# Hybrid attention block: a finer estimate behind the order of the work, deeper pipelines and a new order of the weight tiles

## Chip, core and metric

The kernel runs on one core of a Trainium2 chip. The metric is the device time of one launch in microseconds: the median of three runs. Each profile is one execution of its own; its span runs from the first to the last instruction of the program, and the launch has some 2 us around it.

## What is computed

One block of a hybrid network, in float32, on 512 tokens of width 1024. The input is normalised and multiplied by one wide weight matrix; the product feeds four mixers of width 512, whose gated outputs are multiplied by an output matrix, added to the input and normalised.

```
h = _rmsnorm(x, norm_g)
p_fox, p_ssm, p_nsa, p_mem = _split(h @ w_in, ...)
mem_kv = _rmsnorm(mem, mem_norm_g) @ w_mem_kv
o = concat([_fox_mixer(p_fox), _ssd_mixer(p_ssm), _nsa_mixer(p_nsa), _mem_mixer(p_mem, mem_kv)])
return _rmsnorm(x + o @ w_out, final_norm_g)
```

"Fox" is causal attention of 8 heads with a decay per token. "SSM" is a chunked state-space scan behind a short convolution. "NSA" is causal attention of 8 heads in three branches (compressed, selected and window blocks; with 512 tokens each of the last two covers all earlier keys) under a relative bias. "Mem" is attention of 4 heads over 256 memory tokens. In fox and NSA a softmax row block of 128 queries has 128, 256, 384 or 512 keys.

## The kernel before, in words

**Tiles.** The weights come as 75 tiles of 128x1024 floats, one DMA of 512 KB each on SP's queue. ACT rounds a tile to a high part (`wh`), POOL subtracts it to get the low part (`wl`), and TensorE multiplies high by high, high by low and low by high (`three`, L544). A projection tile is 24 matmuls of 512 columns into one PSUM bank (`pj`, in `tile_a`, L701). `raw`, `wh` and `wl` are rings of three buffers each (L31).

**Mixers.** Each mixer is a `Pipe` (L331): a list of steps and, for each step, stages. Fox has 16 steps (4 head pairs by 4 query blocks), NSA 32 (the two heads of a pair apart). Their stages are: `s1`, the scores and the softmax (TensorE to `pS` and `pW`, DVE, ACT); `s2`, DVE transposes 32x32 blocks inside a tile (`flip`, L1017); `s2o`, four DMAs for each tile write it to DRAM with the blocks turned (`flip_out`, L1030, tiles `fl` to `far`); `s2i`, one DMA for each tile brings it back (`flip_in`, L1043, `far` to `pt`); `s3`, TensorE multiplies `pt` with the values into `pO`; `s4`, DVE gates the result. So a probability tile is turned by way of memory, and TensorE waits for the landing of `pt`. NSA's relative bias also comes by way of memory, once for each of four head pairs: `rows<-rv` from DRAM to DRAM (`spread`, L1146) and `bt<-rows` (`bias_tile`, L1151).

**Order.** There is no run-time scheduler. While the program is written out, `Clock` (L60) keeps an estimated time for each engine; `note` (L126) prices every instruction as it is issued, and `Sched.run` (L301) chooses what to issue next: the first stage, in the order of `PIPES` (L32) and with at most four pipes at once, whose inputs are estimated to be there at TensorE's estimated time; otherwise one step of the next weight tile in `ORDER` (L46), which is the filler. Every engine, SP too, then runs its instructions strictly in that order. If an input comes later than estimated, TensorE stands still, and the filler that could have run stands behind the waiting matmul.

**What `note` counts for a DMA.** It takes 430 ns of SP (720 for a large one to DRAM), then waits its turn on one shared transfer line at 385 GB/s (170 for the large one), and lands 2100 ns later. Any number of DMAs may be under way. A pause of TensorE of over 1700 ns costs 2000 ns more.

**Bounds on running ahead.** A pipe may have `DF`, `DN`, `DM` and `DS` steps (fox, NSA, mem, SSM) between its first and last stage (L26, checked in `Pipe.due`, L342). All share 58 buffers of 128x512 floats (`G`); `RF`, `RM`, `RN`, `RS` (L36) are buffers that projections must leave free for an open pipe. `GF` and `FN` (L29) say at which query blocks the `s3` matmuls are issued: with `FN` of (0, 1, 2, 3), NSA issues block by block. `load` (L425) issues the DMA of a weight tile as soon as the estimated release of its buffer is at most 300 ns ahead of TensorE. `SOON`, `LATER` and `WIDE` (L38) are by how much POOL must be later than DVE before a subtraction goes to DVE.

Of the kernel before, what the change touches and what calls it, by code (L numbers as in the profile page):

```python
# [22 lines left out]
PUMP = 4  # L23
WARM = 12
NL = 3
DF, DM, DN, DS = 7, 3, 6, 3  # L26


GF, FN = 4, (0, 1, 2, 3)  # L29
BACKLOG = 3000  # L30
RAW, RING = 3, 3  # L31
PIPES = "ssm", "cmp", "fox", "pre", "nsa", "mem"  # L32
LAST = 3
ACTIVE = 4

RF, RM, RN, RS = 1, 1, 2, 5  # L36

SOON, LATER, WIDE = 750, 2000, 5750  # L38

TAKES = {"fq": (2, 1), "fk": (2, 1), "fg": (1, 0), "nq": (2, 0), "ng": (1, 0), "z": (1, 0), "mq": (2, 0), "mg": (1, 0),  # L40
         "mk": (1, 0), "ks": (0, 4), "kw": (0, 4), "kc": (1, 1), "vc": (1, 1), "xb": (2, 0), "mv": (4, 0),
# [2 lines left out]
FOX, SSM, NSA, MEM = 0, 2056, 3600, 5416  # L44

ORDER = (  # L46
# [9 lines left out]
)  # L56
KEYS_A = [k for k in ORDER if k[0] not in ("bv", "bc", "mv") and k[0][:2] != "wo"]
# [2 lines left out]
class Clock:  # L60
# [4 lines left out]
    def __init__(self):  # L65
        self.t = dict.fromkeys(("PE", "ACT", "DVE", "POOL", "SP"), 700.0)
        self.dma = 0.0
        self.used = {}
        self.born = {}
        self.port = []  # L70
        self.tiled = False
        self.last = self.landed = 0.0
        self.banks = []

    @staticmethod
# [50 lines left out]
    def note(self, eng, op, a, k):  # L126
        outs = [x for x in (k.get("out", a[0] if a else None), k.get("accum_out")) if self.is_ap(x)]
        ins = [x for x in (*a[(0 if "out" in k else 1):], *[v for n, v in k.items() if n not in ("out", "accum_out")])
               if self.is_ap(x)]
        out = outs[0]  # L130
        start = self.t[eng]
        for x in ins:
            start = max(start, self.at(x, eng))
        for x in outs:
            if not str(x.space).endswith("DRAM"):
                start = max(start, self.at(x, eng, False))
        wide = [x for x in ins if self.size(x) > 1]
        n = max([self.size(x) for x in (out, *wide)])
        port, lag = False, 0
        if eng == "PE":  # L140
            rhs, m = ins[1], self.size(ins[0])
            n = self.size(rhs)
            exact = rhs.dtype == FT and op != "transpose"
            tiled = m <= 64 and exact
            took = max(n * 4 / 2.4, 107) / 2 if tiled else 2 * max(n * 2 / 2.4, 110) if exact else max(n / 2.4 + 13, 110)
            if tiled != self.tiled:
                start += 50 if tiled else 30
                self.tiled = tiled
            if start > self.t[eng] + 1700:
                took += 2000  # L150
        elif op == "dma_start":
            far = self.box(out) == (0, 1, 0, 1) and self.size(out) > 512 * 128
            took = 720 if far else 430
        elif eng == "ACT":
            near = str(wide[0].space).endswith("SB") if wide else True
            took = (110 if near else 55) + 0.83 * n + (305 if "accum_out" in k else 0)
            lag = 95
        elif op == "memset":
            took = 60 + 0.83 * n
        elif eng == "POOL":  # L160
            took = 1000 if n < 16 else 170 + 2.11 * n
            lag = 70
            port = n >= 16
        else:
            near = [x for x in wide if str(x.space).endswith("SB")]
            fast = op in ("tensor_scalar", "tensor_copy") and len(near) == len(wide)
            took = 130 + 0.52 * n if fast else 70 + 1.04 * n
            lag = 85
            if op == "reciprocal":
                took = 70 + 6.4 * n  # L170
            if op == "tensor_tensor_reduce":
                took += 15
                lag = 140
            port = fast or len(near) > 1
        if port:
            start = self.slot(start, took)
        self.t[eng] = start + took
        done = start + took + lag
        if eng == "PE":
            done += self.DRAIN  # L180
        if op == "dma_start":
            nbytes = 4 * self.size(out) * out.ap[0][1]
            self.dma = max(self.dma, done) + nbytes / (170 if took > 430 else 385)
            self.landed = done = self.dma + 2100
            eng = "DMA"
        if op != "dma_start":
            self.last = max(self.last, done)
        for xs, wrote in ((ins, False), (outs, True)):
            for x in xs:
                u = self.used.setdefault(x.name, {})  # L190
                b = self.box(x)
                if wrote:
                    for q in [q for q in u if b[0] <= q[0][0] and q[0][1] <= b[1] and b[2] <= q[0][2] and q[0][3] <= b[3]]:
                        del u[q]
                u[b, eng, wrote] = max(done, u.get((b, eng, wrote), 0.0))
# [135 lines left out]
class Pipe:  # L331
# [10 lines left out]
    def due(self, bg, k):  # L342
        i = self.at[k]
        if i >= len(self.steps) or (k and i >= self.at[k - 1]) or (k == 0 and i - self.at[-1] >= self.depth):
            return math.inf
        t = self.dues.get((k, i), 0.0)
        take = self.takes[k]
        g, b = take(self.steps[i]) if callable(take) else take
        if not bg.room(g + (bg.kept(self) if k == 0 else 0), b):
            return math.inf  # L350
        if k in self.pre:
            keys, tiles = self.pre[k](self.steps[i])
            if any(key not in bg.done for key in keys):
                return math.inf
            t = max(t, bg.clock.ready(tiles()))
        if k == 0:
            t = max(t, max(bg.clock.t["DVE"], bg.clock.t["ACT"]) - BACKLOG)
        return max(t, bg.clock.free_banks(self.banks[k]))

    def run(self, bg, k):  # L360
        i = self.at[k]
# [10 lines left out]
def block_kernel(ctx, tc, I, out):  # L372
# [29 lines left out]
    def PS(name):  # L402
        t = ps.tile([128, 512], FT, name=name, tag="ps", bufs=8)
        clock.bank(t.name)
        return t
# [19 lines left out]
    def load(n, wait=True):  # L425
        while state["load"] < min(n, len(ORDER)):
            i = state["load"]
            free = rings["raw"][1]
            if not wait and free and free[0] > clock.t["PE"] + 300:
                return  # L430
            raw[i] = ring("raw", FT)
            if i < 2:
                for h in range(2):
                    (A if i == h == 0 else Q).dma_start(out=raw[i][:, h * 512:(h + 1) * 512],
                                                        in_=I["wst"][i, :, h * 512:(h + 1) * 512])
            else:
                Q.dma_start(out=raw[i], in_=I["wst"][i])
            state["load"] += 1
# [568 lines left out]
    def rows_by(x, r):  # L1007
        if clock.t["ACT"] + 100 < clock.t["DVE"]:
            A.activation(x, x, AF.Copy, scale=r)
        else:  # L1010
            V.tensor_scalar(out=x, in0=x, scalar1=r, scalar2=None, op0=OP.mult)

    def flips(w):

        return 1 if 2 * w <= 512 else 2

    def flip(tiles, w):  # L1017

        b, per = w // 128, 2 // flips(w)
        made = []  # L1020
        for c in range(0, 2, per):
            t = G("fl", FT, per * w)
            to = t.rearrange("p (j s b x) -> p s b j x", j=4, s=per, b=b)
# [4 lines left out]
        return made, per, w  # L1028

    def flip_out(f):  # L1030
        made, per, w = f
        far = []
        for t in made:
# [7 lines left out]
        return far, per, w  # L1041

    def flip_in(f):  # L1043
        far, per, w = f
        blocks = []
        for m in far:
# [2 lines left out]
            v = t.rearrange("p (i s b x) -> p s b i x", i=4, s=per, b=w // 128)  # L1049
            blocks += [v[:, s, b] for s in range(per) for b in range(w // 128)]  # L1050
        gs.drop(len(far))
        clock.last = clock.landed
        return blocks

    def fox():
# [60 lines left out]
        def p4(s):  # L1116
            return [("fg", s[0])] if s[1] == 3 else [], lambda: []

        return Pipe([(j, b) for j in range(4) for b in range(4)], [s1, s2, s2o, s2i, s3, s4], DF, [2, 0, 0, 0, 1, 0],
                    [(2, 0), (2, 0), (0, 0), (2, 0), (0, 0), (0, 0)], RF, {0: p1, 5: p4})  # L1120

    rv = dr.tile([8, RVW], FT, name="rv")
    rows = [dr.tile([2, 128, RVW], FT, name=f"rows{j}") for j in range(4)]
# [129 lines left out]
    def nsa():  # L1253
# [131 lines left out]
        def p4(s):  # L1385
            return [("ng", s[0])] if s[2] and (s[1] == 3 or s[0] == 3 and LAST == 2) else [], lambda: []

        return Pipe([(j, b, a) for j in range(4) for b in range(4) for a in range(2)], [s1, s2, s2o, s2i, s3, s4],
                    DN, [2, 1, 0, 0, 1, 0], [t1, (2, 0), (0, 0), (2, 0), (0, 0), (2 if LAST == 2 else 0, 0)], RN,
                    {0: p1, 5: p4})  # L1390

    xs = {}
# [53 lines left out]
    pre = []  # L1446
# [433 lines left out]
```

## Time and profile before

| what | value |
|---|---|
| median of three runs | 545.45 us (543.48, 545.45, 547.86) |
| time of the profiled execution | 549.33 us |
| its span | 547.5 us |
| granted TensorE clock, mean over the span | 0.975 |
| TensorE, DVE, ACT, POOL busy | 95%, 67%, 55%, 45% |
| moved by DMA | 90.43 MB |

Every instruction goes through one recording helper, so all of them carry its line, L243, and groups are told apart by the names of their tiles: `pj<-hh,wh` is a projection's matmul, `pt<-far` the DMA that brings a turned tile back. "SPq" is the sequencer of SP, which issues the DMAs. In the lists of waits, "A <- B: total, times, longest" says that A's engine stood still until B was done. Matmuls overlap, so the record of one (390 ns for 512 columns) is longer than the distance to the next (227 ns), and a busy TensorE says little; what counts is its idle time and its clock.

### The profile page before, as it was taken

Reading aid. Unit: us, or ns where it says so; the run is one execution under the profiler, and the core shown is the slowest. Engines: PE = TensorE matmul, PEld = TensorE weight load, DVE = VectorE, ACT = ScalarE, POOL = GpSimd, SP = SyncE. Lnnn points to the kernel's source line nnn. Section 1 sums busy time; section 2 is a strip of 40 time slices with the busy share of each in tenths; the row PEclk is TensorE's granted clock in tenths of the full one; section 3 lists DMA queues with packets and bytes.
Section 4 is the critical chain, followed back from the end, with each engine's and each line's share of the span. In section 5 each row is a group of like instructions: output and inputs, shape, how many; then the busy total and the mean of one; then the engine's idle time right before and its main releaser. Section 6 shows DMA issues by size and latency. Waiting matters only on the chain.

```text
span 547.5 us, 9040 instructions
## 1 busy us (share of the span) xinstructions
PE 519.4 (95%) x2987; PEld 430.2 (79%) x2987; DVE 369.5 (67%) x947; ACT 301.6 (55%) x679; POOL 244.5 (45%) x165
## 2 busy tenths in 40 slices
PE   9999998997999999999998898889999989999995
PEld 5898886886788888877887677778887778878884
DVE  4468698575577777695677778747768668555544
ACT  5754663666466444822346666636556566556333
POOL 3595362333133337757478435213313333263733
PEclk9999998999899999998999999979999999999998
DMA  8772332186476758061227457876865775631303
GB/s 309 299 271 85 116 115 77 27 260 200 119 203 180 227 166 300 39 231 40 77 78 238 142 162 203 249 205 178 248 194 145 225 223 163 198 109 42 113 38 115
DMA packets 70543, 90.43 MB, mean 165 GB/s; under 512 B 26193, under 2 KB 49617, under 8 KB 70497
## 3 DMA queue, kind: packets, MB, share of 16 engines
q1 hardware_dynamic: 70208, 89.40, 52.1%
q8 instruction: 23, 0.38, 0.3%
q10 hardware_dynamic: 288, 0.46, 0.3%
q14 instruction: 24, 0.19, 0.1%
HBM read 71.46 MB, written 20.53 MB: 168 GB/s over the span
## 4 chain that ended last, share of the span: by engine, by line
PE 61%; DVE 16%; DMA 8%; ACT 6%; SPq 4%; issue 3%; POOL 0%; POOLq 0%; DVEq 0%; ACTq 0%
PE pj L243 25%; PE po L243 15%; PE pb L243 6%; PE pO L243 6%; DMA pt<-far 6%; SPq L243 4%; PE pS L243 4%; DVE Rl L243 2%; DVE xs L243 2%; DVE rs L243 2%; ACT pN L243 1%; DMA rows<-rv 1%; DVE ol L243 1%; ACT pF L243 1%; ACT wh L243 1%
## 5 line engine op out<-in xcount | busy, mean ns | idle before, releaser
L243 POOL TENSOR_TENSOR wl<-raw,wh 128x1024 fp32r<-128x1024 f32 (+1 forms) x72 | 172.3, 2397 | 245.2 <-ACT wh L243 201.1
L243 PE MATMUL pj<-hh,wh 128*128 128x512 f32 x352 | 141.4, 402 | 0.0
L243 PE MATMUL pj<-hh,wl 128*128 128x512 f32 x352 | 138.2, 392 | 0.0
L243 PE MATMUL pj<-hl,wh 128*128 128x512 f32 x352 | 138.1, 392 | 0.0
L243 ACT ACTIVATE wh<-raw 128x1024 fp32r<-128x1024 f32 (+1 forms) x72 | 74.1, 1034 | 13.5 <-DMA raw<-in_wst 7.1
L243 PEld LDWEIGHTS pj<-hh,wl 128*128 128x128 f32 x352 | 66.5, 189 | 14.6
L243 PEld LDWEIGHTS pj<-hh,wh 128*128 128x128 f32 x352 | 66.9, 190 | 13.8 <-issue 1.2
L243 PEld LDWEIGHTS pj<-hl,wh 128*128 128x128 f32 x352 | 66.8, 190 | 11.8
L243 ACT ACTIVATE pN<-pN,nm 128x128 f32<-128x128 f32 (+7 forms) x96 | 45.4, 474 | 28.1 <-DVE nm L243 26.6
L243 PE MATMUL po<-wh,oh 128*128 128x512 f32 x96 | 40.1, 418 | 0.0
L243 PE MATMUL po<-wh,ol 128*128 128x512 f32 x96 | 38.1, 397 | 0.0
L243 PE MATMUL po<-wl,oh 128*128 128x512 f32 x96 | 38.0, 396 | 0.0
L243 ACT ACTIVATE pN<-pN,rs 128x128 f32<-128x128 f32 (+3 forms) x32 | 18.0, 564 | 32.4 <-DVE rs L243 32.4
L243 ACT ACTIVATE pF<-pF,nm 128x128 f32<-128x128 f32 (+3 forms) x32 | 17.8, 556 | 30.9 <-DVE nm L243 30.7
L243 DVE TENSOR_SCALAR rs<-sm 128x3 f32<-128x3 f32 x32 | 15.0, 467 | 29.3 <-ACT pN L243 29.3
L243 PE MATMUL pO<-pt,nv 128*64 128x128 f32 x320 | 25.1, 289 | 8.3 <-DMA pt<-far 8.2
L243 DVE TENSOR_TENSOR acc<-acc,po 128x512 f32<-128x512 f32 (+1 forms) x33 | 21.2, 662 | 12.8 <-PE po L243 12.7
L243 PEld LDWEIGHTS pO<-pt,nv 128*64 128x64 f32 x320 | 20.7, 145 | 10.5 <-DMA pt<-far 10.4
L243 DVE STREAM_TRANSPOSE fl<-pN 128x128 f32<-128x128 f32 (+3 forms) x64 | 28.5, 485 | 0.1
L243 DVE CUSTOM_DVE_ANT_0 pN<-pS,bt 128x128 f32<-128x128 f32 (+5 forms) x80 | 22.2, 318 | 8.9 <-PE pS L243 8.1
L243 DVE SCALAR_TENSOR_TENSOR xs<-x,cwh,xs 128x512 f32<-128x512 f32 x24 | 21.1, 879 | 7.8 <-ACT xs L243 7.1
L243 DVE CUSTOM_DVE_ANT_0 pF<-pS,cst 128x128 f32<-128x128 f32 (+3 forms) x32 | 14.4, 482 | 10.9 <-PE pS L243 10.7
(281 smaller groups left out, 1060.6 us busy)
## 6 DMA issues: line engine op xcount, KB each, us to landing
raw<-in_wst SPq DMA_DIRECT2D x73, 512.0 KB, 4.0
far<-fl SPq DMA_DIRECT2D x144, 64.0 KB, 2.5
pt<-far SPq DMA_DIRECT2D x36, 256.0 KB, 4.3
far<-fl SPq DMA_DIRECT2D x96, 48.0 KB, 1.8
pt<-far SPq DMA_DIRECT2D x24, 192.0 KB, 3.4
rows<-rv SPq DMA_DIRECT2D x4, 656.0 KB, 7.2
bt<-rows SPq DMA_DIRECT2D x4, 528.0 KB, 4.6
xn<-in_xn SPq DMA_DIRECT2D x4, 512.0 KB, 7.7
```

Of the source, the lines that this page charges most:

```text
L243: return f(*a, **k)
```

## The change

The instructions that compute are the same, except that some subtractions may move between DVE and POOL and NSA's first query block is multiplied together with the second. The turning still goes by way of memory: the new helper `transposes` (turning on TensorE) is used for widths up to `NARROW`, which is 0, so no step uses it. What changes is:

- the estimate of a DMA: 430 ns of SP for each; it starts only when one of eight lanes is free, taken in turn; data move from 1330 ns after the start, one DMA after the other, at 340 GB/s (less for runs under 512 bytes, 285 for large ones, 235 from DRAM to DRAM); the landing is at the end of that, 1500 ns later for `far` tiles, and the stage after `flip_in` is due another `AFTER` = 500 ns later;
- the estimate of matmuls (a switch between half-width and full-width tiles costs 90 to 100 ns; a pause of TensorE over 1700 ns costs 3300 ns more) and of DVE work that changes partitions;
- `load` waits until the buffer's release is `SLACK` = 1000 ns past;
- depths, reserves and biases, `FN`, the order of the pipes and `ORDER`. The first seven weight tiles stay; the tiles are the same set.

```diff
-DF, DM, DN, DS = 7, 3, 6, 3
+DF, DM, DN, DS = 12, 5, 12, 2
-GF, FN = 4, (0, 1, 2, 3)
+GF, FN = 4, (1, 2, 3,)
-PIPES = "ssm", "cmp", "fox", "pre", "nsa", "mem"
+PIPES = "fox", "pre", "nsa", "ssm", "mem", "cmp"
-RF, RM, RN, RS = 1, 1, 2, 5
-SOON, LATER, WIDE = 750, 2000, 5750
+RF, RM, RN, RS = 3, 2, 3, 5
+SOON, LATER, WIDE = 250, 2750, 8750
+NARROW, AFTER, SLACK = 0, 500, 1000
...
-    ("bv", 0), ("bv", 1), ("bv", 2), ("bv", 3), ("bc", 0), ("bc", 1), ("bc", 2), ("xb", 0), ("fq", 0),
-    ("xb", 4), ("fq", 2), ("fk", 2), ("fk", 1), ("fk", 0), ("xb", 3), ("fq", 1), ("kc", 0), ("xb", 1),
...
+    ("bv", 0), ("bv", 1), ("bv", 2), ("bv", 3), ("bc", 0), ("bc", 1), ("bc", 2), ("fq", 0), ("fq", 3),
+    ("xb", 0), ("fk", 0), ("xb", 5), ("xb", 6), ("z", 3), ("fk", 1), ("z", 2), ("fq", 1), ("fg", 0),
...
-            took = max(n * 4 / 2.4, 107) / 2 if tiled else 2 * max(n * 2 / 2.4, 110) if exact else max(n / 2.4 + 13, 110)
+            took = max(n * 4 / 2.4 + 4, 107) / 2 if tiled else 2 * max(n * 2 / 2.4, 110) if exact else max(n / 2.4 + (16.5 if n >= 500 else 14.5), 110)
             if tiled != self.tiled:
-                start += 50 if tiled else 30
+                start += 90 if tiled else 100
                 self.tiled = tiled
             if start > self.t[eng] + 1700:
-                took += 2000
+                took += 3300
         elif op == "dma_start":
-            far = self.box(out) == (0, 1, 0, 1) and self.size(out) > 512 * 128
-            took = 720 if far else 430
+            took = 430
+            start = max(start, self.lanes.pop(0))
...
-            port = fast or len(near) > 1
+            port = fast or len(near) > 1 and n >= 16
+            if any(self.box(x)[0] != self.box(out)[0] for x in wide):
+                took, lag = took + 90, 12
...
-            nbytes = 4 * self.size(out) * out.ap[0][1]
-            self.dma = max(self.dma, done) + nbytes / (170 if took > 430 else 385)
-            self.landed = done = self.dma + 2100
+            n = out.ap[0][1]
+            for _, c in out.ap[1:]:
+                n *= c
+            run = 4 * min(out.ap[-1][1], ins[0].ap[-1][1])
+            both = str(out.space).endswith("DRAM") and str(ins[0].space).endswith("DRAM")
+            rate = 235 if both else 285 if n > 75000 and run >= 2048 else 340 * min(run, 512) / 512
+            self.dma = max(self.dma, start + 1330) + 4 * n / rate
+            self.landed = done = self.dma + (1500 if any(x.name[:3] == "far" for x in (out, ins[0])) else 0)
+            self.lanes.append(done)
...
-            if not wait and free and free[0] > clock.t["PE"] + 300:
+            if not wait and free and free[0] + SLACK > clock.t["PE"]:
                 return
...
     def flips(w):
...
+        if w <= NARROW:
+            return transposes([t[:, k * 128:(k + 1) * 128] for t in tiles for k in range(b)])
...
     def flip_in(f):
...
-        clock.last = clock.landed
+        clock.last = clock.landed + AFTER
```

More of the change, by code (lines that the diff above doesn't have):

```diff
@@ L71, in __init__ @@
         self.tiled = False
-        self.last = self.landed = 0.0
+        self.last = self.landed = self.sure = 0.0
+        self.lanes = [0.0] * 8
         self.banks = []
@@ L357, in due @@
             t = max(t, max(bg.clock.t["DVE"], bg.clock.t["ACT"]) - BACKLOG)
-        return max(t, bg.clock.free_banks(self.banks[k]))
+        n = self.banks[k]
+        return max(t, bg.clock.free_banks(n(self.steps[i]) if callable(n) else n))
     def run(self, bg, k):
@@ L1011, in rows_by, with transposes @@
             V.tensor_scalar(out=x, in0=x, scalar1=r, scalar2=None, op0=OP.mult)
+    def transposes(blocks):
+        made = []
+        for i in range(0, len(blocks), 4):
+            n = min(4, len(blocks) - i)
+            p = PS("pT")
+            for k in range(n):
+                T.transpose(p[:, k * 128:(k + 1) * 128], blocks[i + k], ident)
+            pt = G("pt", FT, n * 128)
+            evac(pt, p[:, :n * 128])
+            made += [pt[:, k * 128:(k + 1) * 128] for k in range(n)]
+        gs.drop(2)
+        return made
     def flips(w):
@@ L1030, in flip_out @@
     def flip_out(f):
+        if not isinstance(f, tuple):
+            return f
         made, per, w = f
@@ L1043, in flip_in @@
     def flip_in(f):
+        if not isinstance(f, tuple):
+            return f
         far, per, w = f
@@ L1117, in p4 @@
             return [("fg", s[0])] if s[1] == 3 else [], lambda: []
-        return Pipe([(j, b) for j in range(4) for b in range(4)], [s1, s2, s2o, s2i, s3, s4], DF, [2, 0, 0, 0, 1, 0],
-                    [(2, 0), (2, 0), (0, 0), (2, 0), (0, 0), (0, 0)], RF, {0: p1, 5: p4})
+        return Pipe([(j, b) for j in range(4) for b in range(4)], [s1, s2, s2o, s2i, s3, s4], DF, [2, lambda s: s[1] < NARROW // 128, 0, 0, 1, 0],
+                    [(2, 0), (2, 0), (0, 0), lambda s: (2 if s[1] >= NARROW // 128 else 0, 0), (0, 0), (0, 0)], RF, {0: p1, 5: p4})
     rv = dr.tile([8, RVW], FT, name="rv")
@@ L1388, in nsa @@
         return Pipe([(j, b, a) for j in range(4) for b in range(4) for a in range(2)], [s1, s2, s2o, s2i, s3, s4],
-                    DN, [2, 1, 0, 0, 1, 0], [t1, (2, 0), (0, 0), (2, 0), (0, 0), (2 if LAST == 2 else 0, 0)], RN,
+                    DN, [2, 1, 0, 0, 1, 0], [t1, (2, 0), (0, 0), lambda s: (2 if s[1] >= NARROW // 128 else 0, 0), (0, 0), (2 if LAST == 2 else 0, 0)], RN,
                     {0: p1, 5: p4})
```

12 rows, old and new, of the table ORDER are left out of this document.

## The prediction, made before the change was run

> **What bounds the kernel now.** I read the page first, for the engines and the clock, then TensorE's list of waits, then the stretches at half clock, then the DMA issues and the chain around the longest stall. From the page:
>
> ```profile
> span 547.5 us, 9040 instructions
> PE 519.4 (95%) x2987; PEld 430.2 (79%) x2987; DVE 369.5 (67%) x947; ACT 301.6 (55%) x679; POOL 244.5 (45%) x165
> PEclk9999998999899999998999999979999999999998
> ```
>
> TensorE is the bound: busy 519.4 of 547.5 us, all others two thirds or less. The matmuls are given by the work and the change removes none, so only two things can be won: the time in which TensorE stands still, and the slices in which its clock was lowered (the 8s and the 7). What it waits for, from its list of waits:
>
> ```profile
> PE pO L243 <- DMA pt<-far: 11.6, 10, 2.5
> PE pn L243 <- DVE sq L243: 2.1, 1, 2.1
> PE pS L243 <- DVE Rk L243: 1.8, 2, 1.5
> PE pmv L243 <- POOL wl L243: 1.8, 1, 1.8
> PE pT L243 <- DVE pcp L243: 1.7, 2, 1.3
> PE pw L243 <- DVE warm L243: 1.3, 1, 1.3
> PE pS L243 <- DVE Rl L243: 0.6, 2, 0.4
> ```
>
> Without the start (`warm`) these are 11.6 us for turned tiles that land late, and 2.1 + 1.8 + 1.8 + 1.7 + 0.6 = 8.0 us for DVE and POOL. Behind the longer ones the clock falls. The same table of stretches, four of them at half clock, one right after the first for comparison, and the last long stage:
>
> ```profile
> 90.60:97.40 6.80, 6.27 (x17) 0.50 0.07 27
> 97.40:104.20 6.80, 6.80 (x31) 1.00 0.01 2
> 135.00:141.80 6.80, 5.93 (x31) 0.50 0.52 178
> 356.80:363.70 6.90, 5.90 (x41) 0.51 0.58 157
> 247.60:251.00 3.40, 3.40 (x10) 0.50 0.00 0
> 492.00:530.00 38.00, 38.00 (x199) 1.00 0.17 56
> ```
>
> The columns are the length, TensorE's busy time with its matmuls, the granted clock, the DMA share and GB/s. In the first stretch 17 matmuls went through where the next one of the same length has 31. At half clock, half of the busy time is lost: 6.27/2 = 3.1 us, 5.93/2 = 3.0, 5.90/2 = 3.0, 3.40/2 = 1.7, together 10.8 us. The second and third stand behind `pt` (3.0 + 3.0 = 6.0), the first behind `Rk`, the last behind `sq` (3.1 + 1.7 = 4.8). So 11.6 + 8.0 + 10.8 = 30.4 us can be won at most. From 492 us on there is nothing to win: TensorE is busy for 38.00 of 38.00 us at full clock. The stalls themselves, from TensorE's timeline:
>
> ```profile
> 134.65 0.43 PE L243 MATMUL pO<-pt,fv 128*64 128x128 f32 x2 [2.46 <-DMA pt<-far]
> ...
> 247.34 0.24 PE L243 MATMUL pn<-ones,sq 128*128 128x1 f32 x1 [2.07 <-DVE sq L243]
> ...
> 295.46 0.50 PE L243 MATMUL pmv<-wl,mh 128*128 128x512 f32 x1 [1.82 <-POOL wl L243]
> ...
> 354.93 0.43 PE L243 MATMUL pO<-pt,nv 128*64 128x128 f32 x2 [1.06 <-DMA pt<-far]
> 357.80 3.46 PE L243 MATMUL pO<-pt,nv 128*64 128x128 f32 x29 [2.43 <-DMA pt<-far]
> ```
>
> A pause of 2.07 us is followed by 3.4 us at half clock; after one of 1.82 us I find no stretch with a lowered clock. [...]
>
> **Why `pt` is late.** The DMA issues (KB each, median us from issue to landing), then the chain of waits ahead of the stall at 357.80 and SP's own timeline there:
>
> ```profile
> raw<-in_wst SPq DMA_DIRECT2D x73, 512.0 KB, 4.0
> far<-fl SPq DMA_DIRECT2D x144, 64.0 KB, 2.5
> pt<-far SPq DMA_DIRECT2D x36, 256.0 KB, 4.3
> rows<-rv SPq DMA_DIRECT2D x4, 656.0 KB, 7.2
> bt<-rows SPq DMA_DIRECT2D x4, 528.0 KB, 4.6
> ```
>
> ```profile
> 341.65 6.94 DMA rows<-rv
> ...
> 349.98 2.36 SPq L243
> ...
> 352.87 4.89 DMA pt<-far
> ```
>
> ```profile
> 341.65 0.56 SPq L243 DMA_DIRECT2D rows<-rv  x1
> 342.31 6.60 SPq L243 DMA_DIRECT2D far<-fl  x8
> ```
>
> The old estimate has a `pt` of 256 KB land 0.43 + 262144 B/385 GB/s (0.68) + 2.10 = 3.2 us after its issue; the row says 4.3, so TensorE's matmuls on it are placed 1.1 us too early in the median. On top of that SP's queue stands still: eight `far` DMAs behind `rows<-rv` took 6.60 us, the last of them freed when `rows` had landed, and `pt` behind them went out that much later. The old estimate knows no such limit.
>
> **The change part by part**, against the profiled execution (549.33 us, span 547.5).
>
> 1. Later landings, eight lanes. The new estimate of the same `pt` is 1.33 + 262144/340 (0.77) + 1.50 = 3.6, and with the 0.5 of `AFTER` its matmuls are due after 4.1 us, against 4.3. The lanes stop SP in the estimate too. So of the 11.6 us the median lateness of 1.1 falls to 0.2. I take three quarters: 8.7 us (bounds: 0, if other errors set the landings; 11.6). What fills the place is projection matmuls, of which some are left until 492 us (without that cover the whole wait stays). The price is that each tile is held longer, hence the deeper pipes.
>
> 2. The clock behind them. Three quarters of the 6.0 us: 4.5 us (bounds 0 and 6.0).
>
> 3. Stalls on DVE and POOL, 8.0 us and 4.8 us of clock, 12.8 together. The new order is searched with a pause priced at 3.3 us in place of 2.0, close to the 3.0 to 3.1 of the rows, and with dearer DVE work across partitions, which is what `Rk` and `Rl` are. But these waits were in the old search's reach as well. I take half: 6.4 us (bounds 0 and 12.8).
>
> 4. `FN`. NSA's first query block loses its own burst of half-width matmuls, once for each of four pairs. From the timeline:
>
> ```profile
> 318.06 0.40 PE L243 MATMUL po<-wh,ol 128*128 128x512 f32 x1
> 318.39 0.44 PE L243 MATMUL pO<-ct,vcm 96*64 96x128 f32 x4
> 318.66 0.61 PE L243 MATMUL pO<-pt,nv 128*64 128x128 f32 x8
> 319.19 0.50 PE L243 MATMUL po<-wh,oh 128*128 128x512 f32 x1
> 319.53 0.39 PE L243 MATMUL po<-wl,oh 128*128 128x512 f32 x1
> 319.76 0.40 PE L243 MATMUL po<-wh,ol 128*128 128x512 f32 x1
> ...
> 326.08 0.44 PE L243 MATMUL pO<-ct,vcm 96*64 96x128 f32 x4
> 326.35 1.04 PE L243 MATMUL pO<-pt,nv 128*64 128x128 f32 x16
> 327.33 0.34 PE L243 MATMUL pS<-kh,L 128*128 128x160 f32 x1
> ```
>
> Entering costs 318.39 - 318.06 = 0.33 where 0.23 is usual (319.53 to 319.76): 0.10. The burst of 12 takes 0.80, that of 20 takes 1.25, so 0.056 a matmul and 0.13 fixed. The first `po` behind it takes 0.34 against 0.23: 0.11. Together 0.34 us for a burst, four times: 1.4 us (bounds 1 and 2; the matmuls stay).
>
> 5. What the new estimate has too early. A weight tile now lands 1.33 + 524288/285 (1.84) = 3.2 us after its issue, where the row says 4.0 (the old one: 0.43 + 1.36 + 2.10 = 3.9). `rows<-rv` lands after 1.33 + 671744/235 (2.86) = 4.2 against 7.2 (old: 0.72 + 3.95 + 2.10 = 6.8), `bt<-rows` after 1.33 + 540672/285 (1.90) = 3.2 against 4.6. So ACT may stand up to 0.8 us before each `wh`, in front of softmax exponentials in its queue, whose DVE and TensorE successors then wait; POOL's `wl` gets the tile late. `SLACK` adds up to 1.3 us to each load's issue. What covers it: a tile is split two tiles ahead, 24 matmuls of 0.23 us or 5.4 us each. Where the cover is thin, a stall appears like that at 357.80: 2.43 + 3.0 of clock. I take one such, 5.4 us (bounds: 0, cover everywhere; three, 16.2).
>
> 6. Biases. All the `wl` work is on POOL already and a larger `WIDE` keeps it there; `SOON` and `LATER` move some subtractions between two engines with a third or more of their time free. Nothing; uncovered, a few times 0.7 us. `NARROW` of 0 leaves the turning as it is: nothing. Depths and reserves alone run nothing; they let 1 work.
>
> The start up to 42 us has the same seven tiles, and the end from 492 us is full: neither moves.
>
> Sum: -8.7 - 4.5 - 6.4 - 1.4 + 5.4 = -15.6 us, a span of 531.9 and, from 549.33, 533.7 for an execution like the profiled one. The profiled one lies 3.9 us above the median of the runs, 545.45; from that median, 529.9. I predict **530 us**. Its own range, with one stall more or less and half of 3 either way: 521 to 539.
>
> **The rivals.**
>
> *Nearly all stalls go* (0.14). For it: every one of them is an input that the order could have waited for, and filler exists until 492 us. Against it: landings scatter, and no estimate of medians covers them. Time: 545.45 - 30.4 - 1.4 = 514; with a few us left, 517.
>
> *The stalls only move* (0.20). The old order, too, was the best for its estimate, and an order searched hard leans on the estimate wherever that errs. `pt` gets its cover and `wh`, `bt` or DVE lose theirs: terms 1 to 3 give 19.6, and three to four stalls of 5.4 us come in: 545.45 - 19.6 - 1.4 + 16.2 to 21.6 = 541 to 546; I say 543. The same where the finer counts hardly change the order that matters.
>
> *Slower: the pool of 58 buffers fills* (0.14). Twelve NSA steps and twelve fox steps under way, each with up to two tiles, hold up to 48 of 58, beside the operands of the projections; then no projection may start and filler ends in the middle. The estimate sees a full pool but not how late the real engines drain it, since real landings free the buffers. Each time TensorE pauses for a turn of a tile, 2.5 for `far` and 4.3 for `pt`, and loses 3.0 of clock: 9.8 us. It decides from the third time on, with term 1 to 3 won: 545.45 - 19.6 - 1.4 + 3 x 9.8 = 554; I give it 552 to 558. Against it: TensorE's filler lasts to 492 us now, and the reserves went up (1, 1, 2 to 3, 2, 3).
>
> **How the numbers follow.** Forecast 0.52, nearly all 0.14, moved 0.20, pool 0.14. About 1%, 5.5 us, is what can be told from no change: below 540 is faster, above 551 slower. Faster 0.52 + 0.14 = 0.66, same 0.20, slower 0.14. From 516 to 550 lie the forecast, most of the second case and all of the third, over 8 in 10; the bounds of the terms reach from 514 to beyond 555.
>
> **What would show it.** In the changed profile: the wait of `pO` for `pt<-far` down to some 3 us (term 1); at most two or three stretches at half clock ahead of the end, mean clock near 0.985 (terms 2, 3); NSA's first burst of `pO` for each pair has 12 + 20 = 32 matmuls (term 4); `ACT wh` waiting more for `raw<-in_wst` (term 5). It is wrong if `pt` still leads TensorE's waits at 8 us or more, if `wl` or `wh` take its place, or if TensorE pauses for several us with projections held back.

## The result, and the profile after

The changed kernel takes 527.22 us (median of four runs, 526.23 to 528.49), against 546.63 us for the kernel before on the same chip (543.48 to 547.86). The ratio is 0.9655, with a 95% interval of 0.9604 to 0.9705. The profiled execution took 526.90 us with a span of 525.1, 22.4 us less than the span before. The page, in the same rows as before:

```profile
span 525.1 us, 9054 instructions
PE 506.8 (97%) x2987; PEld 422.7 (80%) x2987; DVE 362.3 (69%) x956; ACT 301.7 (57%) x678; POOL 236.7 (45%) x157
PEclk9999999999999999999999999999999999999998
```

The matmuls are as many (2987), and TensorE is still the bound. Its clock is under nine tenths in no slice but the last, in which the matmuls end. TensorE's list of waits after:

```profile
PE pT L255 <- DVE pcp L255: 3.0, 4, 1.4
PE pb L255 <- DVE fv L255: 2.3, 1, 2.3
PE pO L255 <- DMA pt<-far: 2.0, 2, 1.7
PE pj L255 <- POOL wl L255: 1.5, 2, 0.8
PE pw L255 <- DVE warm L255: 1.3, 1, 1.3
PE pmv L255 <- POOL wl L255: 0.9, 1, 0.9
PE pY L255 <- DVE prev L255: 0.4, 1, 0.4
```

The wait for turned tiles went from 11.6 to 2.0 us. The waits for DVE and POOL are as long as they were, 8.1 us in all (8.3 before, with 0.3 us of `pb`), but others: those on `sq`, `Rk` and `Rl` are gone, and a new one of 2.3 us stands in the start. One stretch at half clock is left before the end:

```profile
156.60:160.00 3.40, 3.40 (x14) 0.51 0.43 103
```

It costs 3.40/2 = 1.7 us, where there were 10.8. So of the 22.4 us, 11.6 - 2.0 = 9.6 come from the wait for `pt`, 10.8 - 1.7 = 9.1 from the clock, 0.2 from the other waits. About 1.4 are the four bursts saved by `FN` (below). Some 2 us I cannot place.

### The profile page after: what moved, and what is told of

It is laid out like the page before. It is cut to its first block, busy times and chain, and to the rows that moved or that the text cites. A ratio compares the mean times of both kernels' runs of the same rounds, so it can differ in the third digit from the quotient of the medians.

```text
span 525.1 us, 9054 instructions
## 1 busy us (share of the span) xinstructions
PE 506.8 (97%) x2987; PEld 422.7 (80%) x2987; DVE 362.3 (69%) x956; ACT 301.7 (57%) x678; POOL 236.7 (45%) x157
## 4 chain that ended last, share of the span: by engine, by line
PE 58%; DVE 15%; DMA 12%; issue 5%; ACT 4%; SPq 3%; POOL 2%; POOLq 0%; DVEq 0%; ACTq 0%
PE pj L255 28%; PE po L255 11%; DMA pt<-far 8%; PE pb L255 6%; PE pO L255 4%; ACT pN L255 3%; PE pS L255 3%; SPq L255 3%; DVE rs L255 3%; DVE pN L255 3%; DVE fl L255 2%; DMA raw<-in_wst 2%; POOL wl L255 1%; DMA far<-fl 1%; DVE acc L255 1%
## 5 line engine op out<-in xcount | busy, mean ns | idle before, releaser
L255 DVE TENSOR_SCALAR rs<-sm 128x3 f32<-128x3 f32 x32 | 16.3, 509 | 28.3 <-ACT pN L255 28.3
L255 DVE TENSOR_TENSOR acc<-acc,po 128x512 f32<-128x512 f32 (+1 forms) x33 | 21.0, 662 | 11.9 <-PE po L255 11.7
L255 DVE RECIPROCAL rs<-sm 128x2 f32<-128x2 f32 x24 | 4.0, 166 | 25.4 <-ACT pF L255 16.7
L255 PEld LDWEIGHTS po<-wh,ol 128*128 128x128 f32 x96 | 18.0, 188 | 4.1
L255 PEld LDWEIGHTS po<-wh,oh 128*128 128x128 f32 x96 | 18.1, 188 | 3.3 <-issue 0.3
```

The lines of the kernel that those rows point to most:

```text
L255: return f(*a, **k)
```

## The experiments

All times are medians; the ratio is to runs of the kernel before on the same chip, with its 95% interval. "pt" is TensorE's wait for `pt<-far`, "others" the rest of its list of waits without `warm`, both in us.

| run | what it is | time | ratio | pt | others |
|---|---|---|---|---|---|
| before | | 546.6 | 1 | 11.6 | 8.3 |
| changed | | 527.2 | 0.9655 [0.9604, 0.9705] | 2.0 | 8.1 |
| e1 | before + new estimate | 532.2 | 0.9682 [0.9634, 0.9730] | 2.1 | 11.2 |
| e2 | changed, old estimate | 540.9 | 0.9844 [0.9801, 0.9888] | 13.2 | 4.4 |
| e3 | changed, old DMA prices | 539.7 | 0.9830 [0.9769, 0.9891] | 11.7 | 4.0 |
| e4 | changed, old depths | 543.4 | 0.9878 [0.9822, 0.9935] | 2.8 | 16.7 |
| e5 | before + turned tiles due 1.5 us later | 545.1 | 0.9936 [0.9914, 0.9959] | 7.7 | 12.4 |
| e6 | changed, no lanes | 540.9 | 0.9854 [0.9817, 0.9892] | 6.7 | 10.2 |
| e7 | changed, old load rule | 523.5 | 0.9547 [0.9519, 0.9575] | 0 | 8.7 |
| e8 | changed, old order of tiles | 537.4 | 0.9800 [0.9776, 0.9824] | 0.5 | 15.3 |
| e9 | e7 + earlier evacuation in the start | 519.4 | 0.9487 [0.9451, 0.9524] | 0.8 | 5.8 |
| e10 | e7 + other prices of large loads | 530.0 | 0.9681 [0.9636, 0.9725] | 3.2 | 11.2 |
| e11 | changed, old prices of engines | 526.0 | 0.9619 [0.9566, 0.9672] | 0 | 8.2 |
| e12 | changed, old `FN` | 527.3 | 0.9578 [0.9512, 0.9643] | 2.2 | 7.2 |

The kernel before took 546.6 to 550.8 us on the chips of these runs, so the ratios compare better than the times where they differ by under 1%.

**My theory** was that the estimate of DMAs places TensorE's work on turned tiles where they have landed. **The rival** was that a search fitted a new order to its estimate and the gain is the order's.

### e1 and e2: the estimate alone, and everything but the estimate

e1 puts the class `Clock` of the changed kernel into the kernel before. e2 does the reverse, and sets `AFTER` and the load rule back:

```diff
-NARROW, AFTER, SLACK = 0, 500, 1000
+NARROW, AFTER, SLACK = 0, 0, -300
```

> The kernel before with the new estimate alone (DMA lanes, landings, matmul and DVE prices); its own order, depths, FN and rule for loads stay. Theory (the estimate places the matmuls on turned tiles where the tiles have landed): pO's wait for pt<-far falls from 11.6 us to 3 to 5 even in the old order, and the time to 532 to 540 us. Rival (the gain is that of the searched order, which fits its estimate): with an order not searched for this estimate the stalls only move; 541 to 552 us.

> The changed kernel with the old estimate (all of it, and the old rule for loads, no extra wait after a landing); the new order, depths, reserves, biases and FN stay. Theory: pt<-far leads TensorE's waits again with 8 us or more, two or more stretches at half clock come back, 538 to 550 us. Rival (order and depths carry the gain): 526 to 533 us, pt wait under 5.

e1 took 532.2 us, e2 540.9. The first rows of e1's list of waits, and the first of e2's:

```profile
PE pT L252 <- DVE pcp L252: 3.6, 2, 2.7
PE pb L252 <- DVE fv L252: 2.2, 1, 2.2
PE pO L252 <- DMA pt<-far: 2.1, 3, 1.0
```

```profile
PE pO L246 <- DMA pt<-far: 13.2, 10, 4.5
```

With nothing searched for it, the new estimate takes `pt` from 11.6 to 2.1 us and gives most of the gain: 0.9682 against 0.9655. Without it, the new order and depths bring the wait for `pt` back in full. The theory holds. The rest of the change (order, depths, reserves, biases, `FN`) is worth something too: e2 is 1.6% faster than the kernel before; its other waits are 4.4 us where they were 8.3, and its four stretches at half clock, 3.4 us each, lose 6.8 us where there were 10.8.

### e3 and e11: which half of the estimate

e3 sets only the DMA prices back. e11 sets back only the prices of matmuls, of pauses and of DVE:

```diff
-            took = 430
-            start = max(start, self.lanes.pop(0))
+            far = self.box(out) == (0, 1, 0, 1) and self.size(out) > 512 * 128
+            took = 720 if far else 430
...
-            self.landed = done = self.dma + (1500 if any(x.name[:3] == "far" for x in (out, ins[0])) else 0)
-            self.lanes.append(done)
+            nbytes = 4 * self.size(out) * out.ap[0][1]
+            self.dma = max(self.dma, done) + nbytes / (170 if took > 430 else 385)
+            self.landed = done = self.dma + 2100
```

```diff
...
-                start += 90 if tiled else 100
+                start += 50 if tiled else 30
...
-                took += 3300
+                took += 2000
...
-            if any(self.box(x)[0] != self.box(out)[0] for x in wide):
-                took, lag = took + 90, 12
```

> The changed kernel in which only the estimate of DMAs is the old one (one line at 385 GB/s, landing 2100 ns later, no lanes); prices of matmuls, pauses and DVE, the 500 ns after a landing and the rule for loads stay new. Theory: it is the DMA part that matters: pt wait 6 us or more, 536 to 548 us. Rival (the dearer pause and DVE prices matter as much): 527 to 533 us.

> The changed kernel (527.2 us) in which the prices of matmuls, tile switches, pauses and DVE work are the old ones; the estimate of DMAs is new. Theory (the DMA part carries the gain): pt wait under 4 us, 527 to 533 us. Rival (the dearer pause and the DVE prices hold back the stalls on DVE and POOL, term 3): these waits rise from 8 to 12 us or more, 534 to 542 us.

e3 took 539.7 us, e11 526.0. The longest wait of e3, then the two longest of e11:

```profile
PE pO L249 <- DMA pt<-far: 11.7, 10, 3.3
```

```profile
PE po L253 <- POOL wl L253: 2.2, 1, 2.2
PE pT L253 <- ACT pM L253: 2.1, 1, 2.1
```

The DMA half carries it. With the order kept, the dearer pause and the DVE prices are worth nothing that shows: without them the time is the same, no wait for `pt` is listed, and the other waits add up to 8.2 us for 8.1, though they are others. What these prices did in the search that found the order, no run tests.

### e5 and e6: lateness or lanes

e5 adds only lateness to the kernel before; e6 takes only the lanes from the changed one:

```diff
-        clock.last = clock.landed
+        clock.last = clock.landed + 1500
```

```diff
-            start = max(start, self.lanes.pop(0))
```

> The kernel before with one change: the stage after the load of a turned tile is due 1500 ns after the old estimate of its landing. Theory (lateness of pt alone is most of the gain): pt wait from 11.6 us to 2 to 5, 532 to 540 us. Rival (the eight lanes and the load rule, which keep SP's queue moving, are needed): pt wait stays at 6 or more, 541 us or more.

> The changed kernel with an estimate that lets any number of DMAs be under way; all other prices and the order stay. Theory of lateness: the 500 ns and the 1500 ns still cover the median, 527 to 533 us. Rival (lanes carry it): stalls like the one behind rows<-rv return, pt wait over 6 us, 535 to 545 us.

e5 took 545.1 us, e6 540.9, each with the wait for `pt` that its rival forecast. The rows, e5 first:

```profile
PE pO L243 <- DMA pt<-far: 7.7, 5, 4.2
```

```profile
PE pO L254 <- DMA pt<-far: 6.7, 7, 3.0
```

Five waits of up to 4.2 us remain when every turned tile is due 1.5 us later. The longest, at 358.45 us, has SP's queue standing ahead of it, behind `rows<-rv` as before:

```profile
341.83 7.12 SPq L243 DMA_DIRECT2D far<-fl  x8
```

A lateness of the median does not cover a queue that stands. The lanes are needed, and worth 2.0 points of the ratio; what they would do without the later landing, no run tests. Over all runs of the table, `pt` is 0 to 3.2 us where the estimate has both the lanes and the later landing, whatever the order and the depths, and 6.7 to 13.2 us where it lacks one or both.

### e4 and e8: depths and order

```diff
-DF, DM, DN, DS = 12, 5, 12, 2
+DF, DM, DN, DS = 7, 3, 6, 3
```

e8 puts the list `ORDER` of before into the changed kernel.

> The changed kernel with the depths of before (7, 3, 6, 3 steps for fox, mem, NSA, SSM). Theory: a tile that is due later needs more steps under way; with the old depths scores and softmax are held back and TensorE runs short of steps that keep DVE and ACT fed, pt wait still under 4 us, 530 to 540 us. Rival (depths never bind): 526 to 529 us, the same as the changed kernel.

> The changed kernel with the order of weight tiles of before; estimate, depths, reserves, biases, FN and pipe order are new. Theory (the estimate carries the gain): 528 to 537 us, pt wait under 4 us. Rival (estimate, depths and order only work together, as the old depths with the new order suggest): 540 us or more, with waits of pT on pM or pcp near the end.

e4 took 543.4 us, outside both forecasts; e8 537.4, just over the theory's. For e4, the last two long stages and its longest waits:

```profile
410.00:451.00 41.00, 41.00 (x291) 1.00 0.69 210
451.00:492.00 41.00, 29.03 (x179) 0.83 0.32 87
```

```profile
PE pT L255 <- ACT pM L255: 5.7, 3, 2.4
PE pT L255 <- DVE pcp L255: 4.3, 2, 3.1
```

From 410 to 451 us TensorE is full, and then idle for 12 of 41 us, waiting for the softmax tiles of mem (`pM`) and of NSA's compressed branch (`pcp`). After 451 us ACT has 14 instructions of NSA's softmax (`pN`) left, where the changed kernel has none, and TensorE has 18 projection matmuls (27 in the changed kernel) as filler, all before 470 us. The wait for `pt` stays short, 2.8 us, so it is not the landing that needs the depth. I read it as the spreading of DVE's and ACT's work over the time in which there is filler; which of the four depths does it, no run separates. With the old depths, order and reserves (e1) TensorE is busy for 38.5 of the same 41 us. Each of the two, with the other as before (e4, e8), loses some 8 to 16 us against the changed kernel, by ratios or by times.

### e7: the load rule

```diff
-NARROW, AFTER, SLACK = 0, 500, 1000
+NARROW, AFTER, SLACK = 0, 500, -300
```

> The changed kernel with the old rule for loads (issued when the buffer's release is at most 300 ns ahead). Theory: SP stands in front of raw loads for longer while turned tiles queue behind; 1 to 6 us of the gain go, 528 to 533 us. Rival (SP's queue has time): 525 to 528 us. A third possibility, since nothing was searched for this: stalls only move, to either side.

523.5 us: faster than the changed kernel, which only the third possibility allowed for. Its list of waits has no `pt`:

```profile
PE pT L255 <- DVE pcp L255: 3.5, 4, 1.4
PE pb L255 <- DVE fv L255: 2.4, 1, 2.4
```

The one long wait for `pt` in the changed kernel is this, on SP's timeline and on TensorE's:

```profile
144.00 1.89 SPq L255 DMA_DIRECT2D pt<-far  x4
145.98 0.85 SPq L255 DMA_DIRECT2D raw<-in_wst  x2
146.93 0.86 SPq L255 DMA_DIRECT2D pt<-far  x2
```

```profile
155.31 0.43 PE L255 MATMUL pO<-pt,fv 128*64 128x128 f32 x2 [1.75 <-DMA pt<-far]
155.97 0.33 PE L255 MATMUL pO<-pt,fv 128*64 128x128 f32 x2 [0.23 <-DMA pt<-far]
```

Two weight loads of 512 KB went out together right ahead of the last two turned tiles, whose landing took 8.5 us in the chain of waits. It is tempting to put this down to `SLACK`: the pause of 2.0 us and the half clock behind it (1.7) make 3.7 us, and 527.2 - 523.5 = 3.7. But the match is chance. By the ratios, which compare better here, the difference is 1.1 points, 5.9 us, and in the profiles e7 has 2.0 us less of `pt`, 0.6 more of other waits and as much half clock, now in the start. Nor is the pair gone in e7. SP's queue there at the same place:

```profile
146.16 0.39 SPq L255 DMA_DIRECT2D raw<-in_wst  x1
146.60 0.45 SPq L255 DMA_DIRECT2D pt<-far  x1
147.15 0.38 SPq L255 DMA_DIRECT2D raw<-in_wst  x1
147.57 0.91 SPq L255 DMA_DIRECT2D pt<-far  x2
```

Two loads within a microsecond, and turned tiles behind them; but TensorE comes to these tiles only at 156.34 us, behind projections, and does not wait. Over all its turned tiles e7 has landings that are no shorter: the median is 4.1 us and the longest 10.3, against 3.7 and 9.2 in the changed kernel. In e6, which holds loads back as the changed kernel does, only one load stands between the turned tiles, and the landing took 7.1 us. So the landing is long at this place with one load (7.1) as with two (8.5), and under the old rule the landings are no shorter. That the old rule with this order is faster is shown; by which step, is open.

### e9 and e10: the stall in the start

In the start the list of tiles is the same, but TensorE waited 2.3 us for `fv`. DVE's timeline of the changed kernel:

```profile
30.51 0.73 DVE L255 SCALAR_TENSOR_TENSOR xt<-xt,x,pr 128x512 f32<-128x512 f32 x1
31.17 1.39 DVE L255 TENSOR_SCALAR fv<-pb,rx 128x512 f32<-128x512 f32 x2
```

The same place before the change, where the wait was 0.3 us:

```profile
27.92 1.55 DVE L243 TENSOR_TENSOR hl<-xt,hh 128x512 fp32r<-128x512 f32 x1 [0.54 <-ACT hh L243]
29.40 1.40 DVE L243 TENSOR_SCALAR fv<-pb,rx 128x512 f32<-128x512 f32 x2
```

Now one more normalised tile (`xt`) stands ahead of the evacuation of `pb` (the copy out of PSUM, `fv<-pb`). e9 issues no step of the normalisation in the last two groups of the fourth value tile and the first two of the tile behind it; e10 gives large loads 385 GB/s and a landing 1300 ns after the last byte. Both stand on e7:

```diff
-                if name == "bc" or 1 < i < PUMP:
+                if name == "bc" and (i or n_ > 1) or name == "bv" and (i == 2 or i == 3 and n_ < 4):
```

```diff
-            rate = 235 if both else 285 if n > 75000 and run >= 2048 else 340 * min(run, 512) / 512
+            rate = 235 if both else 385 if n > 75000 and run >= 2048 else 340 * min(run, 512) / 512
...
-            self.landed = done = self.dma + (1500 if any(x.name[:3] == "far" for x in (out, ins[0])) else 0)
+            self.landed = done = self.dma + (1500 if any(x.name[:3] == "far" for x in (out, ins[0])) else 1300)
```

> The changed kernel with the old load rule (523.5 us) and, in the start, no step of the normalisation issued during the last two groups of matmuls of the fourth value tile, so that DVE and ACT empty pb before the fifth normalised tile. Theory (the stall of 2.4 us of pb on fv is DVE's order alone): pb's wait falls to 1 us or less and the stretch at half clock behind it goes, 519 to 522 us. Rival (the normalisation itself is then late and projections wait for it): 523 to 526 us, with pj waiting for hh or hl.

> The changed kernel with the old load rule (523.5 us), and in the estimate large loads move at 385 GB/s and land 1300 ns after their last byte (a weight tile 4.0 us after its issue, not 3.2). Theory (plain loads are estimated too early one by one, and too slow in the bulk at the start): pb's wait for fv halves, ACT waits less for raw, 519 to 524 us. Rival (the order was searched for the other estimate, and any change of it moves stalls about): 526 to 540 us.

e9 took 519.4 us, the fastest of all. On its page no slice is under nine tenths of the clock, and on its list of waits, the second fence, `pb` is gone:

```profile
span 518.9 us, 9056 instructions
PEclk9999999999999999999999999999999999999999
```

```profile
PE pT L255 <- DVE pcp L255: 3.5, 4, 1.4
PE pw L255 <- DVE warm L255: 1.3, 1, 1.3
PE pmv L255 <- POOL wl L255: 0.9, 1, 0.9
PE pO L255 <- DMA pt<-far: 0.8, 2, 0.6
```

e10 does what was expected of it in the start, and loses it elsewhere, as its rival said:

```profile
PE pT L255 <- ACT pM L255: 6.4, 4, 2.3
PE pO L255 <- DMA pt<-far: 3.2, 7, 1.0
...
PE pb L255 <- ACT fv L255: 0.8, 1, 0.8
```

The wait of `pb` is down to 0.8 us by the prices of large loads, rate and landing together, and with all DMA prices of before (e3) it is 0.3. But these prices do not make the stall alone: in e11, which has the new ones beside the old prices of the engines, the extra tile is not ahead of the evacuation either and `pb` waits 0.5 us. It takes both halves of the new estimate. The new estimate has large loads at 285 GB/s; in the start, where they follow one another, they move faster. The stretch from 3 to 19 us of the changed kernel:

```profile
3.00:19.00 16.00, 16.00 (x65) 11.81 (x64) 8.34 (x11) 11.45 (x19) 7.51 (x4) 1.00 1.02 388
```

The last column says 388 GB/s, for all transfers together. So the input of the normalisation may be expected too late, and its steps issued later, ahead of the evacuation; that step is argued, not shown. And a truer price for the loads does not pay with this order: e10 is 6.5 us slower than e7.

### e12: NSA's bursts

```diff
-GF, FN = 4, (1, 2, 3,)
+GF, FN = 4, (0, 1, 2, 3)
```

> The changed kernel (527.2 us) with FN of before, so that NSA's first query block has its own burst of half-width matmuls again; all else stays. Theory (term 4, a burst costs 0.34 us of entering and leaving, four times): 528 to 530 us, stalls as in the changed kernel. Rival (a small edit moves stalls, whose scatter is larger than the term): anywhere from 523 to 536 us, with the difference in the waits and the clock.

527.3 us, against 527.2, and by the ratios 0.8 points less, with intervals that overlap: the runs scatter from 525.2 to 530.2, and the waits differ (`pb` 3.2 in place of 2.3, `pcp` 1.2 in place of 3.0). A term of 1.4 us cannot be read from such a pair. It can be read from the burst itself, in the changed kernel:

```profile
308.98 0.44 PE L255 MATMUL pO<-ct,vcm 96*64 96x128 f32 x4
309.25 0.61 PE L255 MATMUL pO<-pt,nv 128*64 128x128 f32 x8
309.68 0.39 PE L255 MATMUL pO<-ct,vcm 96*64 96x128 f32 x4
309.91 1.04 PE L255 MATMUL pO<-pt,nv 128*64 128x128 f32 x16
310.88 0.34 PE L255 MATMUL pS<-kh,L 128*128 128x160 f32 x1
```

The 32 matmuls take 310.88 - 308.98 = 1.90 us, where the two bursts took 0.80 + 1.25 = 2.05; with one entry (0.10) and one exit (0.11) saved that is 0.36 us, four times 1.4.

## Why the prediction was right, and where it was not

The time was 527.2 us for 530, with 516 to 550 given. In the profiled executions 22.4 us were won where the sum had 15.6, and by the medians 546.63 - 527.22 = 19.4. The sum was taken off 545.45, which is 1.2 us under the median of the kernel before in the runs beside the changed one; that brought the forecast nearer to the result by luck.

**Term 1** (8.7 us) measured 9.6. The reason was half of it. The prediction put the median lateness of 1.1 us first and the standing queue "on top of that". e5 shows lateness alone to be worth 0.6%, and e6 that without the lanes 6.7 us of waiting remain. The eight far DMAs behind `rows<-rv` were the better clue than the median of the landings.

**Term 2** (4.5 us): 6.0 of half clock behind `pt` became 1.7, so 4.3.

**Term 3** (6.4 us): the waits on DVE and POOL did not shrink (8.3 to 8.1), and all 4.8 us of clock behind them went. The sum of the term, 0.2 + 4.8 = 5.0, came out near by this, but its mechanism fell: the term had these waits shrink, and e11 gives no sign that the dearer pause and the DVE prices hold them back. That no pause on DVE was followed by half clock any more is seen; why, is open, and luck is not excluded: the longest of these pauses is no shorter (2.25 us, 2.07 before), and the last section shows that length alone does not decide.

**Term 4** (1.4 us) is right by the rows of the burst, too small for the runs.

**Term 5** (5.4 us lost) is where the sum was most off. ACT's wait for `raw` did not grow; its rows before and after:

```profile
ACT wh L243 <- DMA raw<-in_wst: 7.1, 4, 3.9
```

```profile
ACT wh L255 <- DMA raw<-in_wst: 6.0, 4, 3.9
```

New stalls there are, at 155 us (3.7 with its half clock) and in the start (2.3 us; e9, e10), 6.0 us together; that this is near 5.4 is luck, since neither stands behind a late `wh`. And they are no loss on top: terms 1 to 3 as measured above already contain them. 9.6 + 4.3 + 5.0 + 1.4 = 20.3 us, where the first four terms had 21.0; the 5.4 that the sum then took off accounts for most of what it fell short of 22.4. The step "the start up to 42 us has the same seven tiles ... neither moves" failed: the tiles are the same, but the estimate orders the other engines' work there too.

**The rivals.** The buffer pool never showed itself; deep pipes were not harmful, and with the new order they were needed (e4; e1 does without them). "The stalls only move" did not happen to the change as a whole, yet it is what happens to combinations that nobody searched: e8 has nearly no wait for `pt` left and pays 7.2 us more in other waits than the changed kernel (15.3 for 8.1); e10 has 5.7 us more in both together than e7 (14.4 for 8.7).

## What to carry to other kernels

Where the order of the instructions is fixed by an estimate, the estimate of the transfers decides first: how many may be under way, and what stands behind a long one in the queue, mattered more here than the median landing (e5 won 0.6%, e6 lost 2.0 points). Such an estimate and the order, depths and limits found with it are one thing; change one alone and several us move elsewhere, so a small term is read from the rows, not from a run. Once the large stall is gone, look beside the order: one line in the start and the old load rule gave another 7.8 us (519.4 us, e9).

## What the runs showed of the hardware

A pause of TensorE is not enough to say whether half clock follows. In the changed kernel one of 2.25 us at the start is followed by none (the clock is 1.00 from 32.0 to 38.8 us), and 1.75 with 0.23 soon after it by 3.4 us (0.51 from 156.6 us on). In e7 nearly the same pause in the start, 2.4 us, is followed by this stretch:

```profile
32.10:35.50 3.40, 3.40 (x16) 0.50 1.03 416
```

The stretches at half clock that were measured last 3.3 to 3.4 us (one before, one in the changed kernel, four in e2, two in e4, the one above in e7) or 6.7 to 6.9 (three before, one in e4). What sets these lengths, and why like pauses end differently, no run shows.
